# The second GEMM of the four mlps in seven half-size block products

## The chip, the cores and the metric

The kernel runs on one core of a Trainium2 chip. The metric is the device time of one execution in microseconds (us), the median of the runs shown; lower is better.

## The reference

The program is two transformer-like blocks, one after the other, over 512 tokens of width 1024 in float32. The first has latent attention, a gated linear attention, a merge and a convolutional FFN. The second has four layers, each with a mixer and then a squared-ReLU mlp, and these four mlps are what the change touches:

```python
def _sqrelu_mlp(h, w1, w2):
    return jnp.square(jax.nn.relu(h @ w1)) @ w2

def second_block(x, ...):
    for i in range(DEPTH_2):
        ...
        x = x + mix
        x = x + _sqrelu_mlp(_rmsnorm(x, norm_mlp_g[i]), mlp_w1[i], mlp_w2[i])
    return _rmsnorm(x, final_norm_g)
```

DEPTH_2 is 4, h is 512 x 1024, w1 is 1024 x 4096 and w2 is 4096 x 1024.

## The kernel before

Everything is held with features on the 128 partitions and tokens along the free axis. The residual x stays in SBUF as eight tiles of 128 features x 512 tokens.

Every float32 matmul is made as three matmuls on rounded parts. An operand v is split in a high part hi, rounded by a cast on ScalarE (ACT), and a low part lo = v - hi, made by VectorE (DVE); mm3 (L97 to L101) then adds hi*hi, hi*lo and lo*hi into one PSUM bank. One such matmul has a 128 x 128 stationary operand (a tile of weights) and 512 tokens as the moving one. Weights arrive as raw panels of 128 x 1024 float32 (512 KB) by a DMA of the SP queue into wraw (three buffers), and are split in whi (L83, ACT) and wlo (L85, DVE), three buffers each. `split` (L173 to L182) does the same for activations.

The mlp (L994 to L1026) of one layer goes in four quarters (q), each of 1024 of the 4096 hidden columns. A quarter has a first GEMM of eight column tiles (m), each with one w1 panel and 8 x 3 matmuls; a tile is taken out of PSUM by `evict`: DVE multiplies max(ps, 0) by the norm's factor rb (L1006, tile h), ACT squares it (L1007) and `split` makes its parts hh and hl. Then comes the second GEMM of the quarter, eight column tiles of the output, each with one w2 panel (8 k tiles x 128 columns) and 8 x 3 matmuls with the quarter's eight hh, hl; DVE adds the bank to the tile of x (L1022). In the last quarter of a layer `residual` (L956 to L963) makes that addition (L960) and, for the tile, the operand xh, xl of the next mixer (ACT L948, DVE L949), the square (ACT L191) and its addition to acc_x, on GpSimd (POOL, L194) for all tiles but the last. The last layer makes no operand. GpSimd has no other work in the mlps.

The order of the instructions in each engine's queue is fixed when the program is built, by a framework that sees the dependencies and the buffers; it may put an instruction ahead of one that the code writes before it. There are no due times or costs in the code.

## Time and profile before

| | us |
|---|---|
| median of 3 runs | 3118.34 |
| lowest and highest run | 3111.39, 3121.61 |
| span of the profiled execution, first to last instruction | 3113.3 |
| TensorE (PE) busy in that span | 3029.7 (97%) |
| VectorE (DVE) busy | 1784.0 (57%) |
| ScalarE (ACT) busy | 1222.5 (39%) |
| GpSimd (POOL) busy | 292.5 (9%) |

The profiled execution's own time is its span and what lies around it, which the profile does not show; the median of the runs is 5.0 us above the span. A matmul's record is longer than the distance to the next one, since matmuls are pipelined: where the pace matters, starts are compared. The granted clock is given in shares of TensorE's full speed.

### The profile page before, as it was taken

The numbers are of one execution on the slowest core, as the hardware profiler recorded it, in microseconds if no ns is written. First come the engines' busy times: TensorE is split into PE (matmuls) and PEld (weight loads), VectorE is DVE, ScalarE is ACT, GpSimd is POOL, SyncE is SP. The second block draws the span as 40 slices with busy tenths as digits, with TensorE's granted clock in tenths as the row PEclk, the third lists the DMA queues.
The fourth block names the chain that finished last, engine by engine and source line by source line (L and its number), as shares of the span: only waits on it lengthen the run. The fifth ranks groups of instructions, "written<-read, shape, count | busy, mean of one in ns | idle before, by whom it ended". The sixth has DMA issues, their size and how long they took to land.

```text
span 3113.3 us, 34927 instructions
## 1 busy us (share of the span) xinstructions
PE 3029.7 (97%) x13740; PEld 2493.1 (80%) x13740; DVE 1784.0 (57%) x2444; ACT 1222.5 (39%) x1725; POOL 292.5 (9%) x197
## 2 busy tenths in 40 slices
PE   7999999899999999999999999999999999999998
PEld 4878778678888778888888888888888887788886
DVE  7758795598944974443445344455543459744443
ACT  5336653433333654322344222322322246642222
POOL 3212310100001210000101000100100012100001
PEclk8999999999999999999999999999999999999999
DMA  5571234433332523233322323332233224333322
GB/s 200 190 239 55 80 110 137 168 100 97 95 98 85 137 87 110 95 96 101 109 88 91 99 95 96 101 95 95 95 96 101 95 95 129 91 107 100 96 95 75
DMA packets 108932, 336.67 MB, mean 108 GB/s; under 512 B 12096, under 2 KB 18624, under 8 KB 107744
## 3 DMA queue, kind: packets, MB, share of 16 engines
q1 hardware_dynamic: 99568, 318.13, 32.2%
q10 hardware_dynamic: 9200, 16.32, 1.6%
q8 instruction: 107, 1.75, 0.2%
q14 instruction: 57, 0.47, 0.0%
HBM read 314.22 MB, written 13.63 MB: 105 GB/s over the span
## 4 chain that ended last, share of the span: by engine, by line
PE 79%; DVE 7%; ACT 2%; issue 1%; POOL 1%; DMA 0%; SPq 0%; ACTq 0%; DVEq 0%; POOLq 0%
PE ps L101 25%; PE ps L99 25%; PE ps L100 25%; DVE xc L1094 1%; DVE wlo L85 1%; PE po L120 1%; DVE xc L1168 0%; ACT whi L83 0%; PE pu L766 0%; PE pt L649 0%; DVE tg L1166 0%; PE ps L120 0%; POOL sg L854 0%; POOL yl L182 0%; DVE xc L1167 0%
## 5 line engine op out<-in xcount | busy, mean ns | idle before, releaser
L83 ACT CAST whi<-wraw 128x1024 fp32r<-128x1024 f32 (+3 forms) x523 | 535.4, 1025 | 1492.6 <-PE ps L100 1319.7
L99 PE MATMUL ps<-xh,whi 128*128 128x512 f32 x2224 | 874.6, 395 | 10.1 <-ACT xh L346 6.6
L101 PE MATMUL ps<-xh,wlo 128*128 128x512 f32 x2224 | 875.0, 394 | 5.8 <-DVE wlo L85 5.0
L100 PE MATMUL ps<-xl,whi 128*128 128x512 f32 x2224 | 873.2, 393 | 2.8 <-DVE xl L351 2.8
L85 DVE TENSOR_TENSOR wlo<-wraw,whi 128x1024 fp32r<-128x1024 f32 (+3 forms) x513 | 613.6, 1196 | 244.1 <-ACT whi L83 238.4
L99 PEld LDWEIGHTS ps<-xh,whi 128*128 128x128 f32 x2224 | 421.6, 190 | 97.9 <-ACT xh L346 6.8
L101 PEld LDWEIGHTS ps<-xh,wlo 128*128 128x128 f32 x2224 | 421.1, 189 | 97.5 <-DVE wlo L85 8.5
L100 PEld LDWEIGHTS ps<-xl,whi 128*128 128x128 f32 x2224 | 421.6, 190 | 89.8 <-DVE xl L351 3.5
L101 PE MATMUL ps<-hh,wlo 128*128 128x512 f32 x1200 | 467.2, 389 | 0.0
L100 PE MATMUL ps<-hl,whi 128*128 128x512 f32 x1200 | 467.2, 389 | 0.0
L99 PE MATMUL ps<-hh,whi 128*128 128x512 f32 x1200 | 467.2, 389 | 0.0
L1006 DVE SCALAR_TENSOR_TENSOR h<-ps,rb 128x512 f32<-128x512 f32 x128 | 88.1, 691 | 321.4 <-PE ps L101 321.4
L194 POOL TENSOR_TENSOR acc_x<-acc_x,sq 128x512 f32<-128x512 f32 x54 | 87.5, 1620 | 1959.6 <-ACT sq L191 1959.6
L99 PEld LDWEIGHTS ps<-hh,whi 128*128 128x128 f32 x1200 | 225.3, 188 | 46.8
L100 PEld LDWEIGHTS ps<-hl,whi 128*128 128x128 f32 x1200 | 225.3, 188 | 46.6
L101 PEld LDWEIGHTS ps<-hh,wlo 128*128 128x128 f32 x1200 | 225.3, 188 | 46.5
L1022 DVE TENSOR_TENSOR x<-ps,x 128x512 f32<-128x512 f32 x96 | 66.4, 692 | 314.2 <-PE ps L101 314.2
L101 PE MATMUL ps<-yh,wlo 128*128 128x512 f32 x360 | 140.9, 392 | 3.9 <-DVE wlo L85 3.9
L99 PE MATMUL ps<-yh,whi 128*128 128x512 f32 x360 | 140.9, 391 | 0.8 <-DVE sg L853 0.5
L100 PE MATMUL ps<-yl,whi 128*128 128x512 f32 x360 | 140.8, 391 | 0.4 <-DVE yl L182 0.4
L960 DVE TENSOR_TENSOR x<-ps,x 128x512 f32<-128x512 f32 x64 | 44.2, 691 | 163.0 <-PE ps L101 162.8
L907 DVE SCALAR_TENSOR_TENSOR cacc<-pad,vecs,cacc 128x512 f32<-128x512 f32 x176 | 131.5, 750 | 4.3
(401 smaller groups left out, 3140.9 us busy)
## 6 DMA issues: line engine op xcount, KB each, us to landing
wraw<-in_w SPq DMA_DIRECT2D x256, 512.0 KB, 3.5
wraw<-in_w_up SPq DMA_DIRECT2D x44, 512.0 KB, 3.4
wraw<-in_a_w_in SPq DMA_DIRECT2D x40, 512.0 KB, 3.5
wraw<-in_w_ada SPq DMA_DIRECT2D x32, 512.0 KB, 3.9
wraw<-in_w_in SPq DMA_DIRECT2D x29, 512.0 KB, 3.5
wraw<-in_c_w_in SPq DMA_DIRECT2D x24, 512.0 KB, 3.4
wraw<-in_a_w_out SPq DMA_DIRECT2D x32, 320.0 KB, 2.8
adaw<-in_w_ada SPq DMA_DIRECT2D x8, 1024.0 KB, 9.4
```

Source lines behind the costliest of these rows:

```text
L83: nc.scalar.copy(hi[:, :n], raw[:, :n])
L85: e.tensor_tensor(lo[:, :n], raw[:, :n], hi[:, :n].bitcast(F32), ALU.subtract)
L99: mm(out, wh, xh, start=start, stop=False)
L100: mm(out, wh, xl, start=False, stop=False)
L101: mm(out, wl, xh, start=False, stop=stop)
L120: ops = [self.nc.tensor.matmul(*o, start=i == 0, stop=i == last) for i, o in enumerate(ops)]
L194: (nc.vector if k == last else eng or nc.gpsimd).tensor_tensor(acc, acc, s, ALU.add)
L907: nc.vector.scalar_tensor_tensor(av, src, w, av, ALU.mult, ALU.add)
L960: nc.vector.tensor_tensor(xm, ps, xm, ALU.add)
L1006: nc.vector.scalar_tensor_tensor(h, ps, 0.0, self.rb, ALU.max, ALU.mult)
L1022: nc.vector.tensor_tensor(self.x[:, m, :], ps, self.x[:, m, :], ALU.add)
L1094: nc.vector.scalar_tensor_tensor(xm, t[:, k:k + T], w(k), xm, ALU.mult, ALU.add)
```

## The change

The second GEMM of a quarter is made in pairs of output column tiles (m, m + 1). For such a pair the output is a 2 x 2 block matrix: two column tiles by two halves of 256 tokens. The quarter's eight k tiles make four k-pairs, an even and an odd tile, and so w2 is a 2 x 2 block of two k halves by two column tiles. Strassen's scheme in Winograd's form makes the four output blocks of seven block products in place of eight. A block product (`product`) is four k-pairs x 3 matmuls of 256 tokens.

- Operands of the activations (`quad`): from the two tiles of a k-pair, cut into four halves H, four differences t are made on GpSimd (one behind the even tile, three behind the odd one); seven blocks (B11, T1, B21, B22, T3, T2, T4) are split into hh and hl by ACT and DVE.
- Operands of the weights (`Feed`): from the two raw panels a and b of a pair GpSimd makes four sums of 512 columns (`sum`, tile ssum, one buffer). Split are panel a (chunk 0), ssum's first half (chunk 1), its second half (chunk 2), and the second half of panel b (the tail, tiles thi and tlo). w2 is laid out on the host with the even k tiles ahead of the odd ones.
- Evictions (`pair`): three PSUM banks A, E and D. Three partial results are copied to SBUF (u) by ACT; GpSimd adds u to x in two steps ("u", 512 columns, and "d", 256), and DVE adds four banks of 256 columns to x.
- `Feed.pump` writes the loads and splits of coming panels behind each tile or product; the first pair of a quarter goes through its products in the order 1526374, the others in 1265734.
- In a layer's last quarter `residual` is called for both tiles behind each pair, without an addition of its own.

```diff
+TH = T // 2
+EVEN_ODD = [0, 2, 4, 6, 1, 3, 5, 7]
+B11, T1, B21, B22, T3, T2, T4 = range(7)
...
+class Feed:
+    USES = {"1": (0, 0), "2": (0, 1), "6": (1, 0), "5": (1, 1), "7": (2, 0), "3": (2, 1), "4": (3, 0)}
+    LEFT = {0: "12", 1: "65", 2: "73"}
...
+    def pump(self):
+        k, nc = self.k, self.k.nc
+        moved = True
+        while moved:
+            moved = False
+            if self.loaded < len(self.order) and self.loaded - self.read < k.raw_bufs:
+                n, src = self.order[self.loaded]
+                t = k.wp.tile([P, PANEL], F32, tag="wraw", name=k.nm("wraw"), bufs=k.raw_bufs)
+                nc.sync.dma_start(t, src)
+                self.raw.setdefault(n, []).append(t)
+                self.loaded += 1
+                moved = True
+                continue
+            if self.made < len(self.chunks):
+                n, c = self.chunks[self.made]
+                pair = self.items[n][0] == "pair"
+                if len(self.raw.get(n, ())) == (2 if pair else 1) and (
+                        self.made < k.hl_bufs or self.made - k.hl_bufs in self.freed):
+                    if pair and c == 0:
+                        self.sum(n)
+                    src = self.raw[n][0] if c == 0 else self.sums[n][:, 2 * c - 2:2 * c, :].rearrange("p s c -> p (s c)")
+                    hi = k.wp.tile([P, PANEL], F32R, tag="whi", name=k.nm("whi"), bufs=k.hl_bufs)
+                    lo = k.wp.tile([P, PANEL], F32R, tag="wlo", name=k.nm("wlo"), bufs=k.hl_bufs)
+                    k.split(hi, lo, src)
+                    self.got[n, c] = (self.made, hi, lo)
+                    self.made += 1
+                    if not pair:
+                        self.read += 1
+                    moved = True
+                    continue
+            if self.tails and self.tail_free and self.got.get((self.tails[0], 2)):
+                n = self.tails.pop(0)
+                hi, lo = [self.pool.tile([P, 512], F32R, tag=t, name=k.nm(t), bufs=1) for t in ("thi", "tlo")]
+                k.split(hi, lo, self.raw[n][1][:, 512:])
+                self.got[n, 3] = (None, hi, lo)
+                self.tail_free = False
+                self.read += 2
+                moved = True
+    def sum(self, n):
+        k = self.k
+        t = self.sums[n] = self.pool.tile([P, 4, 512], F32, tag="ssum", name=k.nm("ssum"), bufs=1)
+        a, b = self.raw[n]
+        tt = lambda o, x, y, op: k.nc.gpsimd.tensor_tensor(t[:, o, :], x, y, op)
+        tt(1, b[:, :512], b[:, 512:], ALU.add)
+        tt(0, t[:, 1, :], a[:, :512], ALU.subtract)
+        tt(2, a[:, :512], b[:, :512], ALU.subtract)
+        tt(3, a[:, 512:], t[:, 0, :], ALU.subtract)
...
+    def done(self, p):
+        self.used.add(p)
+        for c, ps in self.LEFT.items():
+            if p in ps and self.used.issuperset(ps):
+                self.freed.add(self.got[self.at, c][0])
+        if p == "4":
+            self.tail_free = True
+        if len(self.used) == 7:
+            self.used = set()
+            self.at += 1
...
+    def quad(self, hi, lo, H, pool, part):
+        nc = self.nc
+        t = self.quad_t = pool.tile([P, 4, TH], F32, tag="qt", name=self.nm("qt"), bufs=1) if part == 0 else self.quad_t
+        sub = lambda i, a, b: nc.gpsimd.tensor_tensor(t[:, i, :], a, b, ALU.subtract)
+        if part == 0:
+            sub(0, H[:, 1, :], H[:, 0, :])
+            self.split(hi[:, B11, :], lo[:, B11, :], H[:, 0, :])
+            self.split(hi[:, T1, :], lo[:, T1, :], t[:, 0, :])
+        else:
+            sub(2, H[:, 3, :], t[:, 0, :])
+            sub(1, H[:, 3, :], H[:, 1, :])
+            sub(3, H[:, 2, :], t[:, 2, :])
+            self.split(hi[:, B21:B22 + 1, :], lo[:, B21:B22 + 1, :], H[:, 2:4, :])
+            self.split(hi[:, T3:T4 + 1, :], lo[:, T3:T4 + 1, :], t[:, 1:4, :])
+    def product(self, ps, w, ops, i, start):
+        wh, wl = w
+        mm, last = self.nc.tensor.matmul, len(ops) - 1
+        for j, (xh, xl) in enumerate(ops):
+            c = slice(j * P, (j + 1) * P)
+            mm(ps, wh[:, c], xh[:, i, :], start=start and j == 0, stop=False, skip_group_check=not start)
+            mm(ps, wh[:, c], xl[:, i, :], start=False, stop=False, skip_group_check=not start)
+            mm(ps, wl[:, c], xh[:, i, :], start=False, stop=j == last, skip_group_check=not start)
+    def pair(self, feed, ops, psp, pool, put, first=False):
+        nc = self.nc
+        A, E, D = [self.bank(psp)[:, :TH] for _ in range(3)]
+        u = pool.tile([P, 3, TH], F32, tag="u", name=self.nm("u"), bufs=2)
+        plan = {"1": (A, B11, True), "2": (E, B21, True), "6": (A, T2, False), "5": (D, T1, True),
+                "7": (A, T3, False), "3": (D, B22, False), "4": (A, T4, False)}
+        for p in "1526374" if first else "1265734":
+            ps, i, start = plan[p]
+            self.product(ps, feed.weights(p), ops, i, start)
+            feed.pump()
+            if p == "1":
+                nc.scalar.copy(u[:, 0, :], A)
+            elif p == "6":
+                nc.scalar.copy(u[:, 1, :], A)
+                put("u", None, u[:, 0:2, :])
+            elif p == "5":
+                nc.scalar.copy(u[:, 2, :], D)
+                put("d", None, u[:, 2, :])
+            elif p == "2":
+                put("11", E, u[:, 0, :])
+            elif p == "7":
+                put("22", A, u[:, 2, :])
+            elif p == "3":
+                put("12", D, u[:, 1, :])
+            else:
+                put("21", A, None)
+            feed.done(p)
...
     def residual(self, m, ps, g, pool, last=False):
         nc = self.nc
         xm = self.x[:, m, :]
-        nc.vector.tensor_tensor(xm, ps, xm, ALU.add)
+        if ps is not None:
+            nc.vector.tensor_tensor(xm, ps, xm, ALU.add)
         if not last:
             self.operand(m, g)
         self.sq_last = self.sq_add(self.acc, m, KD - 1, xm, pool, T, apart=last)
...
     def mlp(self, i, psp, sp, g_next):
-        nc, A, tc = self.nc, self.A, self.tc
+        nc, A = self.nc, self.A
         with self.pool(name="ml", bufs=1) as mp:
+            w2 = lambda m, q: A["w2"][i, m, :, q * PANEL:(q + 1) * PANEL]
+            feed = Feed(self, mp, [it for q in range(4) for it in
+                                   [("panel", A["w1"][i, 8 * q + m]) for m in range(8)]
+                                   + [("pair", w2(m, q), w2(m + 1, q)) for m in range(0, 8, 2)]])
+            feed.pump()
             for q in range(4):
-                hs = []
+                ops = []
                 for m in range(8):
-                    pan = self.panel_k(A["w1"][i, 8 * q + m], KD)
-                    ps = psp.tile([P, 512], F32, tag="mm", name=self.nm("ps"))
-                    self.gemm(ps, pan, self.xh, self.xl, KD)
-
-                    def evict(ps=ps, hs=hs):
-                        h = mp.tile([P, T], F32, tag="h32", name=self.nm("h32"), bufs=3)
+                    hi, lo = feed.panel()
+                    ps = self.bank(psp)
+                    self.gemm(ps, [(hi, lo, k * P) for k in range(KD)], self.xh, self.xl, KD)
+                    feed.pump()
+                    def evict(ps=ps, m=m, ops=ops):
+                        if m % 2 == 0:
+                            self.H = mp.tile([P, 4, TH], F32, tag="H", name=self.nm("H"), bufs=2)
+                            ops.append([mp.tile([P, 7, TH], F32R, tag=t, name=self.nm(t), bufs=4) for t in ("hh", "hl")])
+                        h = self.H[:, 2 * (m % 2):2 * (m % 2) + 2, :].rearrange("p a t -> p (a t)")
                         nc.vector.scalar_tensor_tensor(h, ps, 0.0, self.rb, ALU.max, ALU.mult)
                         nc.scalar.activation(h, h, AF.Square)
-                        hh = mp.tile([P, T], F32R, tag="hh", name=self.nm("hh"), bufs=16)
-                        hl = mp.tile([P, T], F32R, tag="hl", name=self.nm("hl"), bufs=16)
-                        self.split(hh, hl, h)
-                        hs.append((hh, hl))
+                        self.quad(*ops[-1], self.H, mp, m % 2)
                     self.when(evict)
                     self.step()
-                for m in range(8):
-                    hi, lo = self.panel(A["w2"][i, m, :, q * PANEL:(q + 1) * PANEL], PANEL)
-                    ps = psp.tile([P, 512], F32, tag="mm", name=self.nm("ps"))
-                    for k in range(8):
-                        ks = slice(k * P, (k + 1) * P)
-                        self.mm3(ps, hi[:, ks], lo[:, ks], hs[k][0], hs[k][1], k == 0, k == 7)
-                    if q < 3:
-                        nc.vector.tensor_tensor(self.x[:, m, :], ps, self.x[:, m, :], ALU.add)
-                    else:
-                        self.residual(m, ps, g_next(m) if g_next else None, sp, last=g_next is None)
+                    feed.panel_done()
+                for m in range(0, 8, 2):
+                    x = self.x[:, m:m + 2, :].rearrange("p m (h t) -> p (m h) t", h=2)
+                    def put(what, ps, u, x=x):
+                        if what == "u":
+                            nc.gpsimd.tensor_tensor(x[:, 0:2, :], x[:, 0:2, :], u, ALU.add)
+                        elif what == "d":
+                            nc.gpsimd.tensor_tensor(x[:, 3, :], x[:, 3, :], u, ALU.add)
+                        else:
+                            n = ("11", "12", "21", "22").index(what)
+                            nc.vector.tensor_tensor(x[:, n, :], ps, x[:, n, :], ALU.add)
+                    self.pair(feed, ops, psp, mp, put, first=m == 0)
+                    if q == 3:
+                        for mm in (m, m + 1):
+                            self.residual(mm, None, g_next(mm) if g_next else None, sp, last=g_next is None)
...
-    A["w2"] = np.stack([_tiles(a["mlp_w2_2"][j]) for j in range(4)])
+    w2 = np.stack([_tiles(a["mlp_w2_2"][j]) for j in range(4)])
+    A["w2"] = w2.reshape(4, 8, P, 4, 8, P)[:, :, :, :, EVEN_ODD].reshape(w2.shape)
```

The first GEMM, the mixers and the first block are as before.

## Rows read from the trace of the kernel before

**Rows 1.** The page's busy times: us, share of the span, instructions.

```profile
PE 3029.7 (97%) x13740; PEld 2493.1 (80%) x13740; DVE 1784.0 (57%) x2444; ACT 1222.5 (39%) x1725; POOL 292.5 (9%) x197
```

**Rows 2.** Stretches of layer 0's mlp: second GEMM, first GEMM, the layer's last second GEMM.

```profile
core 0: us, PE busy (x) PEld busy (x) DVE busy (x) ACT busy (x) POOL busy (x), PEclk, DMA share, GB/s
...
1239.60:1283.10 43.50, 43.50 (x193) 36.06 (x192) 15.33 (x16) 8.44 (x8) 0.00 (x0) 1.00 0.31 97
1283.10:1326.60 43.50, 43.50 (x193) 36.05 (x193) 20.55 (x24) 17.66 (x24) 0.00 (x0) 1.00 0.30 97
...
1500.70:1544.20 43.50, 43.50 (x193) 36.05 (x193) 22.46 (x26) 17.60 (x24) 10.75 (x6) 1.00 0.37 122
```

**Rows 3.** Instruction groups by shape, the weight load: count, busy us, mean ns.

```profile
L99 PEld LDWEIGHTS ps<-hh,whi 128*128 128x128 f32 x1200 | 225.3, 188 | 46.8
```

**Rows 4.** Timeline of PE, one second-GEMM tile's first matmul and the next's.

```profile
1239.62 0.39 PE L99 MATMUL ps<-hh,whi 128*128 128x512 f32 x1
...
1245.07 0.39 PE L99 MATMUL ps<-hh,whi 128*128 128x512 f32 x1
```

**Rows 5.** Timeline of PE, first and last of 24 matmuls of 256 columns.

```profile
170.53 0.28 PE L99 MATMUL ps<-ch,whi 128*128 128x256 f32 x1
...
173.29 0.28 PE L101 MATMUL ps<-ch,wlo 128*128 128x256 f32 x1
```

**Rows 6.** Timeline of all engines around the end of a first-GEMM tile.

```profile
1212.40 1.06 ACT L83 CAST whi<-wraw 128x1024 fp32r<-128x1024 f32 x1 [3.20 <-PE ps L100]
1212.42 0.39 PE L99 MATMUL ps<-xh,whi 128*128 128x512 f32 x1
...
1212.62 0.69 DVE L1006 SCALAR_TENSOR_TENSOR h<-ps,rb 128x512 f32<-128x512 f32 x1 [2.70 <-PE ps L101]
...
1213.35 0.63 ACT L1007 ACTIVATE h<-h 128x512 f32<-128x512 f32 x1
1213.49 1.23 DVE L85 TENSOR_TENSOR wlo<-wraw,whi 128x1024 fp32r<-128x1024 f32 x1 [0.17 <-ACT whi L83]
...
1214.01 0.62 ACT L176 CAST hh<-h 128x512 fp32r<-128x512 f32 x1
```

**Rows 7.** Instruction groups by shape, ACT.

```profile
L83 ACT CAST whi<-wraw 128x768 fp32r<-128x768 f32 x12 | 10.1, 838 | 26.2 <-PE ps L100 24.4 <-issue 0.9 <-ACT stage L426 0.5
...
L652 ACT CAST Th<-pt 128x256 fp32r<-128x256 f32 x32 | 12.0, 377 | 0.0
```

**Rows 8.** Instruction groups by shape, DVE.

```profile
L1022 DVE TENSOR_TENSOR x<-ps,x 128x512 f32<-128x512 f32 x96 | 66.4, 692 | 314.2 <-PE ps L101 314.2
...
L653 DVE TENSOR_TENSOR Tl<-pt,Th 128x256 fp32r<-128x256 f32 x32 | 13.2, 413 | 0.2
```

**Rows 9.** Timeline of POOL: an addition of 512 columns, eight of 256.

```profile
1157.55 1.28 POOL L194 TENSOR_TENSOR acc_x<-acc_x,sq 128x512 f32<-128x512 f32 x1 [5.54 <-ACT sq L191]
...
78.62 6.16 POOL L340 TENSOR_TENSOR xa<-xa,acc 128x256 f32<-128x256 f32 x8 [14.86 <-ACT acc L163]
```

**Rows 10.** Timeline of all engines in layer 3's mixer, DVE and POOL.

```profile
2620.20 1.56 POOL L182 TENSOR_TENSOR yl<-xc,yh 128x512 fp32r<-128x512 f32 x1 [15.90 <-ACT yh L176]
...
2620.52 0.68 DVE L1089 TENSOR_TENSOR xpad<-ps,rb 128x512 f32<-128x512 f32 x1
...
2621.12 1.72 DVE L85 TENSOR_TENSOR wlo<-wraw,whi 128x1024 fp32r<-128x1024 f32 x1
```

**Rows 11.** Timeline of all engines in layer 0's last second GEMM.

```profile
1513.83 0.75 DVE L949 SCALAR_TENSOR_TENSOR xl<-x,vecs,xh 128x512 fp32r<-128x512 f32 x1
...
1513.94 1.78 POOL L194 TENSOR_TENSOR acc_x<-acc_x,sq 128x512 f32<-128x512 f32 x1 [3.66 <-ACT sq L191]
```

**Rows 12.** Timelines of POOL and of DVE in one stretch of the first block.

```profile
52.13 11.63 POOL L317 TENSOR_TENSOR adas<-adas,adaw 128x512 f32<-128x512 f32 x7 [1.30 <-ACT adaw L316]
...
54.40 6.89 DVE L314 SCALAR_TENSOR_TENSOR adas<-adaw,s,adas 128x512 f32<-128x512 f32 x4
```

**Rows 13.** DMA issues: count, KB each, median us to landing.

```profile
wraw<-in_w SPq DMA_DIRECT2D x256, 512.0 KB, 3.5
```

More of the change, by code (lines that the diff above doesn't have):

```diff
@@ L50, with __init__, panel, panel_done @@
 NV = _n
+class Feed:
+    USES = {"1": (0, 0), "2": (0, 1), "6": (1, 0), "5": (1, 1), "7": (2, 0), "3": (2, 1), "4": (3, 0)}
+    LEFT = {0: "12", 1: "65", 2: "73"}
+    def __init__(self, k, pool, items):
+        self.k, self.pool, self.items = k, pool, items
+        self.loaded, self.read = 0, 0
+        self.chunks = []
+        for n, it in enumerate(items):
+            self.chunks += [(n, c) for c in ((0, 1, 2) if it[0] == "pair" else (0,))]
+        self.made, self.freed = 0, set()
+        self.order = [(n, s) for n, it in enumerate(items) for s in it[1:]]
+        self.raw, self.sums, self.got = {}, {}, {}
+        self.lastsum = -1
+        self.tails = [n for n, it in enumerate(items) if it[0] == "pair"]
+        self.tail_free = True
+        self.at, self.used = 0, set()
+    def pump(self):
[45 more added lines that the diff above has]
+        tt(3, a[:, 512:], t[:, 0, :], ALU.subtract)
+    def panel(self):
+        i, hi, lo = self.got[self.at, 0]
+        return hi, lo
+    def panel_done(self):
+        self.freed.add(self.got[self.at, 0][0])
+        self.at += 1
+    def weights(self, p):
+        c, h = self.USES[p]
+        _, hi, lo = self.got[self.at, c]
+        s = slice(512 * h, 512 * h + 512)
+        return hi[:, s], lo[:, s]
+    def done(self, p):
[4 more added lines that the diff above has]
+        if p == "4":
+            self.tail_free = True
+        if len(self.used) == 7:
+            self.used = set()
+            self.at += 1
```

## The prediction

> **What bounds the kernel now.** I read the page's busy table first, then the stretches of one mlp layer, then the instructions around one tile's end. TensorE has work for 97% of the span [rows 1]. The four mlps are where the change lies. In layer 0 one quarter's second GEMM takes 43.50 us, the next first GEMM 43.50 us; layer 0's last second GEMM, with the residual work added, is 43.50 us too [rows 2]. In all three TensorE is busy throughout at a granted clock of 1.00, the upper level of 2.4 GHz; VectorE (DVE) has 15 to 22 us of work there, ScalarE (ACT) 8 to 18, GpSimd (POOL) none or 10.75. So in the mlps the matmul stream is the bound, with no gap. What counts is the time from start to start, not the length of a record: 24 matmuls of 512 columns take 5.45 us, 0.2267 us each [rows 4], while a record lasts 0.39; a weight load of 188 ns [rows 3] fits below it.
>
> **What falls away.** Per quarter (one of 16: four layers of four) the second GEMM has 8 x 8 x 3 = 192 matmuls of 512 columns: 192 x 0.2267 = 43.5 us, as [rows 2] shows. Afterwards it is 4 pairs x 7 products x 4 k-pairs x 3 = 336 matmuls of 256 columns. The trace has such a stream: 23 steps of 256 columns, each with a weight load of its own, take 173.29 - 170.53 = 2.76 us, 0.120 us each [rows 5]. So the load, longer than a step, still doesn't set the pace. 336 x 0.120 = 40.3 us: 3.2 us less per quarter, **-51 us** in all. A product is 1.44 us, a pair 10.08.
>
> The Trainium skill ("TensorE: Matmul & The Clock Gate", Back-to-back issue gap) puts the gap at the columns over 2.4 GHz plus some 2.5 ns. By it the steps would be 216 and 109 ns (estimates from that page) and the gain 663 - 587 = 76 us; both rows lie above it, by 11 ns each, and since matmuls of half the width are twice as many, the row takes 25 us off the gain. The rows decide.
>
> **What is added, and where it can hide.** ACT has 8.44 + 17.66 = 26 us per quarter now [rows 2]; 12 copies u out of PSUM (0.38, as the 128x256 copy in [rows 7]) add 4.6, casts of 3.5 panels per pair in place of 2 (1.05) 6.3, operands of 7 x 256 columns for 4 x 256 some 4: 41 of 84 us. DVE has 36 [rows 2]; six more lo of a panel (1.23, [rows 6]) 7.4, operands some 5, sixteen additions of half a tile (0.41, as the 128x256 row of [rows 8]) for eight of 0.69 another 1: 49. Both stay below TensorE, so by busy share alone they are hidden. POOL goes from next to nothing to 16 subtractions of 256 columns (0.77 each), 16 sums of 512 (1.28), 4 x (u 1.28, d 0.77): 41 us [rows 9]. The w2 layout is made on the host; DMAs stay 512 KB and land in 3.5 us [rows 13]; of eight PSUM banks a pair holds three. These cost nothing as long as that slack stands.
>
> What is not free is DVE and POOL side by side. In [rows 10] POOL's subtraction starts at 2620.20 and ends at 2621.76; DVE's xpad (one operand in PSUM) runs beside it in its usual 0.68; the wlo that follows (both operands in SBUF) is issued at 2621.12 and ends at 2622.84, 1.08 us after POOL's end. The reverse is in [rows 11]: POOL, issued 0.11 us behind an SBUF-SBUF operation of DVE, takes 1.78 in place of 1.28. In [rows 12] seven POOL additions need 11.63 us, and four DVE operations among them 6.89: 1.72 us for one of each. They take turns. The Trainium skill ("SBUF — State Buffer", Who interferes with whom) says so: GpSimd's SBUF reads and VectorE's second SBUF operand share one port, and the second to issue is held until the first ends. The trace agrees, and this is the rule that speaks against the change.
>
> So I count turns. A pair needs of POOL 4 x 1.28 (sums) + 1.28 + 0.77 = 7.2 us, of DVE three lo of 1024 (1.08) and one of 512 (0.44, the 1.72 less 1.28) = 3.7. In sum 10.9, some 0.3 less with handovers overlapped as in [rows 12]: I take 10.6, against 10.08 of TensorE. The additions out of PSUM don't count. The first GEMM has room (per two tiles 3.1 of POOL and some 4 of DVE in 10.9 us), and there the first pair is made in advance.
>
> *Start of a second GEMM.* Let 0 be the start of its first matmul; [rows 6] has the same moment at 1212.42. ACT casts the panel whose buffer comes free (there at 1212.40), DVE's h comes, ACT's square ends at 1.56, the cast's lo on DVE runs from 1.07 to 2.2. POOL's three subtractions for the last operands need H complete: 1.6, held to 2.2 by that lo; ended at 3.0; held by the lo of B21 and B22 to 3.5; ended at 5.0. Then ACT's cast of three parts (0.84, [rows 7]) to 5.9, and its lo on DVE, 0.86 (three quarters of 1.14, as 1024 columns start to start), behind a POOL operation that has begun meanwhile: 7.6. The fourth product (T2) wants the last k-pair's lo at 3 x 1.44 + 9 x 0.12 + 0.12 = 5.5. Stall 2.1 us, x 16 = **+34**. Bounds: 0.3 with no turns (1.6 + 2.3 + 0.84 + 0.86 + gaps), 3.4 if a coming panel's cast and lo are put ahead: +5 to +54. B21's lo, ready at 3.5, is wanted at 4.0: hidden.
>
> *The pairs.* The sum buffer is single, so sum n+1 starts when chunk 2 of n is split. Chunk 2 of pair 1 is ready at about 15.8; then one pair per 10.6: pair 3's at 37.0. Its fifth product wants it at 3 x 10.08 + 4 x 1.44 + 2.1 = 38.1. It holds, with 1.1 us to spare: **0**. Bounds 0 to +2 per quarter (12 quarters, +24).
>
> *The last quarter of a layer.* Here come per pair two POOL additions of squares (1.28) and two DVE xl (0.44 to 0.6): 3.5 us of turns; before the change they had POOL idle around them [rows 2, 11]. The residuals of pairs 0 and 1 fall before pair 3's chunk 2: 7.0 - 1.1 = 5.9 us of stall; in the last layer, which makes no operand, 5.1 - 1.1 = 4.0. 3 x 5.9 + 4.0 = **+22**; bounds 0 (they run after the last sum) to twice that, +43.
>
> **Sum.** -51 + 34 + 0 + 22 = +5 on the profiled span of 3113.3: 3118. The median of the runs, 3118.34, lies 5.0 above that span; I add it: **3122 us**. A change of 0.3%, 9 us, is about what a measurement of this kernel can tell from none.
>
> **Rivals.**
> *The turns fall into gaps* (faster). If POOL's work finds DVE idle (DVE is needed 49 of 84 us) and the additions of squares wait behind the last sum, the stall at the start shrinks to some 0.8 and the last quarter costs nothing: -51 + 13 = -38, 3080 to 3090. For it: the budget is over by only 5%, and [rows 12] is the densest place of the trace. Against: both directions of [rows 10, 11]. It decides where a pair's turns come below 10.08.
> *The single sum buffer* (slower). Nothing uses the port while ACT casts chunk 2 (1.06 and a hand-over), and the next sum waits: 11.9 per pair, chunk 2 of pair 3 at 39.6, 1.5 us of stall in 12 quarters and 2.5 more in 4: +28, 3150. It decides above 11.2 per pair.
> *The queues as written* (much slower). If the second raw panel of pair n+1 is fetched only after the tail of n is split, the chain is 3.5 (DMA) + 5.1 (sums) + 2.1 (u, d) + additions and two lo, near 15: 8 us a quarter, +126, 3245. Against: in [rows 6] a coming panel's cast stands ahead of the eviction, so queues are ordered by what is ready.
> *A narrow step at half the wide one* (faster), 0.2267 / 2 = 0.113 in place of 0.120: 5376 x 0.0066 = 36 us more gain on TensorE, but turns bound the pairs, so that about 20 of it would be seen: 3100. Against: [rows 5]. The page's gap, 109 ns, goes the same way.
>
> **Chances.** The sum as it stands (3105 to 3140) 0.35; gaps 0.30; sum buffer 0.24; queues as written 0.08; half step 0.03. Faster: 0.30 + 0.03 + 0.02 of the first; same: 0.21 of it; slower: 0.24 + 0.08 + 0.12 of it. The bounds give -51 + 5 = -46 (3072) to -51 + 54 + 24 + 43 = +70 (3188); the range is 3075 to 3190, the likeliest case's own 3105 to 3140.
>
> **What would show it.** Right: steps of 0.120 in the products; a gap of about 2 us before the fourth product of each quarter, ended by DVE's lo; POOL's busy time up from 292 [rows 1] by 650 us or more, 512-column sums well above 1.28 on the mean, DVE's lo of 1024 above 1.23; last quarters some 5 us longer than the others. Wrong: no gaps, sums at 1.3; or TensorE waiting in every pair for a lo made from ssum; or a step of 256 columns away from 0.120, which would move the whole sum by 5.4 us per ns.

## The result and the profile after

The changed kernel takes 3283.0 us (median of 4 runs, 3280.9 to 3285.5) against 3117.6 for the kernel before: a ratio of 1.0531, 95% interval 1.0516 to 1.0546. The forecast was 3122 us, its range ended at 3190: the size was off by 161 us. Of the three signs, slower had been given the largest chance, 0.44.

The page's busy times of the kernel after answer to [rows 1]; line numbers are now those of the changed kernel:

```profile
PE 3049.4 (93%) x16044; PEld 2597.7 (79%) x16044; DVE 2140.6 (65%) x2828; ACT 1452.8 (44%) x2173; POOL 1142.1 (35%) x837
```

TensorE's share fell from 97% to 93%: a gap has opened, while VectorE and GpSimd are far from full on the mean. The stretches, as in [rows 2], are the four second GEMMs of layer 0 and the last one of layer 3, each from its first product to the next block's first matmul:

```profile
core 0: us, PE busy (x) PEld busy (x) DVE busy (x) ACT busy (x) POOL busy (x), PEclk, DMA share, GB/s
1236.83:1289.31 52.48, 43.27 (x337) 40.98 (x336) 32.82 (x38) 22.67 (x34) 34.92 (x24) 1.00 0.25 79
1332.86:1384.44 51.58, 43.00 (x338) 40.92 (x336) 31.44 (x37) 22.30 (x34) 34.90 (x24) 1.00 0.26 81
1427.99:1479.55 51.56, 43.03 (x338) 40.95 (x337) 31.37 (x37) 22.30 (x34) 34.88 (x24) 1.00 0.27 81
1523.09:1582.96 59.87, 48.32 (x338) 46.06 (x336) 40.76 (x43) 30.30 (x48) 43.05 (x29) 0.89 0.23 69
3207.45:3264.55 57.10, 47.07 (x337) 44.88 (x335) 29.98 (x35) 24.04 (x39) 42.05 (x30) 0.91 0.10 28
```

Each was 43.5 before. The other layers repeat this: the twelve quarters that are not a layer's last sum to 623.0 us, 100.8 more than 12 x 43.52; the four last ones to 236.8, 62.7 more. That is 163.4 of the 165.7 us by which the profiled spans differ (3279.0 - 3113.3); the first GEMMs are as long as before.

The list of waits, with TensorE's product lines (engine, line, what it waited for: us, times, longest) and the links behind them:

```profile
PE ps L223 <- DVE x L1194: 63.5, 57, 3.7
PE ps L223 <- ACT u L242: 44.2, 16, 2.8
PE ps L224 <- DVE hl L342: 24.7, 48, 0.8
...
DVE x L1194 <- POOL x L1191: 43.9, 47, 3.1
POOL ssum L123 <- DVE wlo L342: 61.1, 27, 3.5
ACT whi L336 <- POOL ssum L123: 61.6, 20, 3.4
```

L1194 is a block's addition out of PSUM, L242 the copy u1, L1191 the addition "d", L1189 "u", L123 the sums, L336 and L342 the casts and the lo parts. The wait that the forecast put first, on hl at the start, is the smallest of these three. TensorE's list has no wait for a lo part made from ssum, the one for which the forecast had looked in the pairs.

**One quarter from the inside**, the second of layer 0. TensorE's matmuls that waited:

```profile
1334.52 0.39 PE L224 MATMUL ps<-hl,whi 128*128 128x256 f32 x1 [0.30 <-DVE hl L342]
1338.03 0.39 PE L224 MATMUL ps<-hl,whi 128*128 128x256 f32 x1 [0.39 <-DVE hl L342]
1340.18 0.38 PE L223 MATMUL ps<-hh,whi 128*128 128x256 f32 x1 [0.57 <-ACT hh L336]
1341.37 0.39 PE L224 MATMUL ps<-hl,whi 128*128 128x256 f32 x1 [0.80 <-DVE hl L342]
1346.06 0.39 PE L223 MATMUL ps<-hh,whi 128*128 128x256 f32 x1 [2.76 <-ACT u L242]
1349.65 0.39 PE L223 MATMUL ps<-hh,thi 128*128 128x256 f32 x1 [1.30 <-DVE x L1194]
1360.71 0.38 PE L223 MATMUL ps<-hh,thi 128*128 128x256 f32 x1 [1.19 <-DVE x L1194]
```

Counted from start to start less the step of 0.12, the first four are 0.46 + 0.55 + 0.73 + 1.06 = 2.8 us: the start that was forecast at 2.1. The fifth, 2.92, is product 7, which adds into bank A and must wait until the copy u1 has read it. The others are product 4 of each pair (its weights are thi), which adds into A after "22" has read it: 1.46, 1.35, 1.08, 0.51, 4.4 in sum. With 40.3 of steps this makes 50.4 of 51.58; the rest is in gaps under 0.25.

Why is A read so late? ScalarE, GpSimd and VectorE in the same quarter:

```profile
1344.69 1.04 ACT L336 CAST whi<-ssum 128x1024 fp32r<-128x1024 f32 x1 [3.35 <-POOL ssum L123]
1345.64 0.36 ACT L242 COPY u<-ps 128x256 f32<-128x256 f32 x1
```

```profile
1350.80 1.30 POOL L123 TENSOR_TENSOR ssum<-wraw 128x512 f32<-128x512 f32 x1 [2.00 <-DVE wlo L342]
1352.06 1.75 POOL L123 TENSOR_TENSOR ssum<-wraw,wraw 128x512 f32<-128x512 f32 x1
1353.77 1.29 POOL L123 TENSOR_TENSOR ssum<-ssum,wraw 128x512 f32<-128x512 f32 x1
1355.14 2.16 POOL L123 TENSOR_TENSOR ssum<-wraw,ssum 128x512 f32<-128x512 f32 x1
1357.26 1.27 POOL L1189 TENSOR_TENSOR x<-x,u 128x512 f32<-128x512 f32 x1
1358.49 1.71 POOL L1191 TENSOR_TENSOR x<-x,u 128x256 f32<-128x256 f32 x1
1362.20 1.29 POOL L123 TENSOR_TENSOR ssum<-wraw 128x512 f32<-128x512 f32 x1 [2.00 <-DVE wlo L342]
```

```profile
1360.23 0.76 DVE L1194 TENSOR_TENSOR x<-ps,x 128x256 f32<-128x256 f32 x2 [0.62 <-POOL x L1191]
1360.90 1.21 DVE L342 TENSOR_TENSOR wlo<-ssum,whi 128x1024 fp32r<-128x1024 f32 x1
```

The copy u1 stands on ScalarE behind a cast that waits 3.35 us for a sum. On GpSimd the next pair's four sums stand ahead of this pair's u and d. "22" adds to the same quarter of x as d and waits for it; behind "22" and "12" stands chunk 2's lo part, and that frees the one sum buffer, for which the next sums wait. It is a ring: 11.40 us from one pair's first sum to the next's, 1350.80 to 1362.20, where the products need 10.08.

### The profile page after: what moved, and what is told of

Its sections match the earlier page's. It is cut to its first block, busy times and chain, and to the rows that moved or that the text cites. A ratio compares the mean times of both kernels' runs of the same rounds, so it can differ in the third digit from the quotient of the medians.

```text
span 3279.0 us, 41343 instructions
## 1 busy us (share of the span) xinstructions
PE 3049.4 (93%) x16044; PEld 2597.7 (79%) x16044; DVE 2140.6 (65%) x2828; ACT 1452.8 (44%) x2173; POOL 1142.1 (35%) x837
## 4 chain that ended last, share of the span: by engine, by line
PE 48%; POOL 22%; DVE 10%; ACT 5%; issue 5%; DMA 2%; POOLq 0%; DVEq 0%; SPq 0%; ACTq 0%
PE ps L259 13%; PE ps L260 13%; PE ps L261 13%; POOL ssum L123 13%; POOL qt L204 3%; POOL x L1189 2%; POOL x L1191 2%; PE ps L223 2%; DMA wraw<-in_w 2%; DVE wlo L342 2%; PE ps L224 2%; PE ps L225 1%; DVE H L1176 1%; ACT H L1177 1%; DVE x L1194 1%
## 5 line engine op out<-in xcount | busy, mean ns | idle before, releaser
L259 PE MATMUL ps<-xh,whi 128*128 128x512 f32 x2224 | 872.7, 394 | 10.6 <-ACT xh L506 5.8
L185 ACT CAST whi<-wraw 128x1024 fp32r<-128x1024 f32 (+2 forms) x267 | 265.1, 995 | 563.9 <-PE ps L260 404.7
L223 PE MATMUL ps<-hh,whi 128*128 128x256 f32 x1536 | 451.5, 294 | 55.8 <-ACT u L242 44.2
L224 PE MATMUL ps<-hl,whi 128*128 128x256 f32 x1536 | 447.2, 291 | 24.7 <-DVE hl L342 24.7
L225 PE MATMUL ps<-hh,wlo 128*128 128x256 f32 x1536 | 441.0, 287 | 0.0
L187 DVE TENSOR_TENSOR wlo<-wraw,whi 128x1024 fp32r<-128x1024 f32 (+2 forms) x257 | 299.8, 1166 | 194.8 <-ACT whi L185 193.3
L336 ACT CAST whi<-wraw 128x1024 fp32r<-128x1024 f32 (+1 forms) x208 | 208.1, 1004 | 251.3 <-PE ps L260 160.9
L342 DVE TENSOR_TENSOR wlo<-wraw,whi 128x1024 fp32r<-128x1024 f32 (+1 forms) x208 | 275.3, 1325 | 66.3 <-ACT whi L336 66.3
L342 DVE TENSOR_TENSOR wlo<-ssum,whi 128x1024 fp32r<-128x1024 f32 x128 | 188.2, 1470 | 77.8 <-ACT whi L336 77.6
L204 POOL TENSOR_TENSOR qt<-H 128x256 f32<-128x256 f32 x128 | 135.8, 1061 | 282.6 <-ACT H L1177 282.6
L342 DVE TENSOR_TENSOR hl<-qt,hh 128x256 fp32r<-128x256 f32 (+1 forms) x128 | 93.2, 728 | 183.5 <-ACT hh L336 183.5
L336 ACT CAST whi<-ssum 128x1024 fp32r<-128x1024 f32 x128 | 133.9, 1046 | 167.6 <-POOL ssum L123 61.6
L336 ACT CAST hh<-qt 128x256 fp32r<-128x256 f32 (+1 forms) x128 | 79.3, 620 | 268.9 <-POOL qt L204 268.9
```

Of the source, the lines that this page charges most:

```text
L185: nc.scalar.copy(hi[:, :n], raw[:, :n])
L187: e.tensor_tensor(lo[:, :n], raw[:, :n], hi[:, :n].bitcast(F32), ALU.subtract)
L204: sub = lambda i, a, b: nc.gpsimd.tensor_tensor(t[:, i, :], a, b, ALU.subtract)
L223: mm(ps, wh[:, c], xh[:, i, :], start=start and j == 0, stop=False, skip_group_check=not start)
L224: mm(ps, wh[:, c], xl[:, i, :], start=False, stop=False, skip_group_check=not start)
L225: mm(ps, wl[:, c], xh[:, i, :], start=False, stop=j == last, skip_group_check=not start)
```

## The experiments

Kernels e1 to e17 are the changed kernel with edits; "before" was timed beside each on the same chip. Two columns give the length of a quarter in us, read from TensorE's timeline as above: the third and the last of layer 1 (layers are counted from 0). Where the next tile's matmuls are mixed into the last quarter, it can't be read so (-).

```
                            us      ratio [95%]                third  last
before                    3117.6                               43.5   43.5
changed                   3283.0  1.0531 [1.0516, 1.0546]      51.57  59.89
e1_puts_dve               3228.1  1.0356 [1.0341, 1.0372]      46.84  53.65
e2_copies_first           3279.8  1.0522 [1.0504, 1.0539]      52.34  59.87
e3_no_sums                3137.1  1.0063 [1.0048, 1.0078]      44.72  45.00
e4_ssum2                  3259.4  1.0455 [1.0437, 1.0472]      50.62  56.48
e5_puts_copies            3261.1  1.0463 [1.0445, 1.0480]      49.59  55.55
e6_sums_dve               3184.6  1.0219 [1.0202, 1.0236]      46.85  50.81
e7_sums_copies_quad       3162.3  1.0147 [1.0125, 1.0170]      45.32  48.66
e8_bank4                  3104.9  0.9970 [0.9954, 0.9987]      41.05  46.97
e9_order_pool_sums        3172.8  1.0181 [1.0168, 1.0195]      44.55  54.01
e10_acc_dve               3091.3  0.9924 [0.9910, 0.9938]      41.05  -
e11_first_order           3098.4  0.9944 [0.9931, 0.9956]      40.71  46.45
e12_classic_last          3091.8  0.9925 [0.9912, 0.9937]      41.06  43.52
e13_shadow_sums           3282.3  1.0535 [1.0518, 1.0553]      52.69  58.22
e14_best_strassen         3083.4  0.9899 [0.9884, 0.9913]      40.72  -
e15_best_mixed            3086.8  0.9908 [0.9893, 0.9922]      40.72  43.52
e16_shadow_clean          3230.6  1.0358 [1.0342, 1.0373]      48.30  55.26
e17_all_quads             3086.6  0.9900 [0.9884, 0.9917]      40.72  -
```

**e1, u and d off GpSimd's queue.**

```diff
 if what == "u":
-    nc.gpsimd.tensor_tensor(x[:, 0:2, :], x[:, 0:2, :], u, ALU.add)
+    nc.vector.tensor_tensor(x[:, 0:2, :], x[:, 0:2, :], u, ALU.add)
 elif what == "d":
-    nc.gpsimd.tensor_tensor(x[:, 3, :], x[:, 3, :], u, ALU.add)
+    nc.vector.tensor_tensor(x[:, 3, :], x[:, 3, :], u, ALU.add)
```

> The two additions of copied products to x ("u", "d") go from GpSimd to VectorE; nothing else changes. Theory A (order in the queues): block "22" reads bank A only after "d", and "d" stands on GpSimd behind the four sums of the next pair; with it gone from that queue, TensorE's waits on VectorE's L1194 before product 4 (64 us of PE's, 1.0 to 1.5 us in each pair after the first) nearly vanish: 3215 to 3240 us. Theory B (the two engines only take turns at SBUF, their work adds up): the sum of the work is the same, so 3270 to 3300 us, and the waits only change their names.

3228.1 us, 55 us less: in theory A's range. But the run does not part order from length, as theory B's "the sum of the work is the same" did not hold. On the mean u and d took 1.65 and 1.28 us on GpSimd and take 1.23 and 0.70 on VectorE: 1.0 us a pair less, some 63 us in 64 pairs. A kernel with u and d ahead of the next sums on GpSimd, order alone, was not run. The waits on L1194 fell from 63.5 to 34.9 us rather than to nothing: d now stands on VectorE, behind lo parts.

**e2 and e5, the copy u1 ahead of the cast.** e2 moves the copies in the code; e5 is e1 with the order stated as well:

```diff
+    if p in "165":
+        self.ucopy = nc.scalar.copy(u[:, "165".index(p), :], D if p == "5" else A)
     feed.pump()
-    if p == "1":
-        nc.scalar.copy(u[:, 0, :], A)
...
-    k.split(hi, lo, src)
+    cast = k.split(hi, lo, src)
+    if k.ucopy is not None:
+        k.after(k.ucopy, cast)
```

> ScalarE's copies of banks A and D (u0, u1, u2) are issued before the casts of the weight chunks that the same product frees, instead of behind them. Theory A: the wait of 2.8 us before product 7 of every quarter's first pair (44 us in 16 quarters) is a copy of 0.38 us that stands behind a cast which waits for a sum; it goes, and 25 to 45 us come back: 3238 to 3258 us. Theory B (the sums themselves are late, whoever waits for them): the next product waits for the same chunk instead, under 12 us come back.

> As e1_puts_dve, and with the copies of banks held ahead of the casts by a stated order on ScalarE (e2 changed only where the code writes them, and the order that was built kept u1 behind the cast). Theory A: with u1 out from behind the cast that waits for a sum, the 2.0 to 2.15 us before product 7 of a quarter's first pair go, 32 us in 16 quarters: 3195 to 3205 us, if nothing else is late there. Rival (chunk 1 of the next pair is late by as much): 3218 to 3230 us.

e2 changed nothing, because ScalarE's order did not change: its timeline (the copies are now L240) still has the cast that waits ahead of u1:

```profile
1338.10 1.04 ACT L337 CAST whi<-ssum 128x1024 fp32r<-128x1024 f32 x1 [3.34 <-POOL ssum L123]
1339.05 0.36 ACT L240 COPY u<-ps 128x256 f32<-128x256 f32 x1
```

e5 missed: 33 us slower than e1. The wait on u1 is gone, but the cast of the first pair's chunk 2 now stands behind copies too. Its lo part frees the sum buffer later, and the next sum starts 9.4 us into the second quarter (1344.60 - 1335.24), 6.4 in e1. Chunk 1's lo part waits for that sum, and "22" stands behind it on VectorE:

```profile
1351.04 1.33 DVE L347 TENSOR_TENSOR wlo<-ssum,whi 128x1024 fp32r<-128x1024 f32 x1 [2.27 <-ACT whi L341]
1352.29 0.74 DVE L1200 TENSOR_TENSOR x<-ps,x 128x256 f32<-128x256 f32 x2
```

From the next pair on the sums wait for transfers: 125 of the 181 us that they wait in e5, against 20 in the changed kernel. So with sums on GpSimd one late place passes its lateness to the next; removing the wait on u1 did not bring what it showed.

**e3, no sums; e4, two sum buffers.**

```diff
# e3
-    if pair and c == 0:
-        self.sum(n)
-    src = self.raw[n][0] if c == 0 else self.sums[n][:, 2 * c - 2:2 * c, :].rearrange("p s c -> p (s c)")
+    src = self.raw[n][0] if c == 0 else self.raw[n][c - 1]
# e4
-    t = self.sums[n] = self.pool.tile([P, 4, 512], F32, tag="ssum", name=k.nm("ssum"), bufs=1)
+    t = self.sums[n] = self.pool.tile([P, 4, 512], F32, tag="ssum", name=k.nm("ssum"), bufs=2)
```

> Leaves out GpSimd's four sums of weight blocks per pair; chunks 1 and 2 are split from the raw panels instead, so the casts, the lo parts, the transfers and all matmuls stay (the output is not the reference's). Theory A and B alike: what is left is the start of each quarter (2.1 to 2.8 us, 16 of them), and the last quarters' residual work: 3150 to 3185 us. Theory C (most of the excess is the start stall, the quads and the clock): 3230 us or more, as the sums are not what product 4 and 7 wait for.

> The sums get two buffers. The ring as read from the trace (sums, u, d, the block puts, chunk 2's lo part, which frees the buffer: 11.4 us for a pair of 10.1) is opened at its last link; the order in GpSimd's queue stays. Theory A, ring by way of the buffer: a pair falls to 10.1 to 10.5 us in the first three quarters: 3220 to 3250 us. Rival (GpSimd's own queue is the ring: sums 6.4, u 1.3, d 1.7, with turns at the port): a pair stays over 11 us, 3265 to 3285 us.

e3, which leaves the sums out, fell below the expected range: 146 of the 166 us go. The start of a quarter shrinks from 2.8 to 1.1 us, and the last quarters, whose residual work is all still there, cost 0.3 us more than the others in place of 8.3. Yet e3 is still slower than the kernel before, at 44.7 us a quarter: "22" out of A costs 0.5 us a pair even so.

e4 brought 23.6 us, between its two expectations: the buffer is one link of the ring, and opening it leaves u and d behind the sums. In its second quarter the wait before product 7 is gone and those before product 4 fell from 4.4 to 3.2 us, but the start grew from 2.8 to 4.7: the second pair's sums now stand on GpSimd ahead of the last k-pair's differences.

**e6 to e9, where the sums are made, and the order around them.** Each adds to the one before; e9 is e8 with the sums back on GpSimd and u and d on VectorE.

```diff
# e6
-    tt = lambda o, x, y, op: k.nc.gpsimd.tensor_tensor(t[:, o, :], x, y, op)
+    tt = lambda o, x, y, op: k.nc.vector.tensor_tensor(t[:, o, :], x, y, op)
# e7: the copies' order as in e5, and the differences of a quarter's last tile
-    sub = lambda i, a, b: nc.gpsimd.tensor_tensor(t[:, i, :], a, b, ALU.subtract)
+    sub = lambda i, a, b: (nc.vector if last else nc.gpsimd).tensor_tensor(t[:, i, :], a, b, ALU.subtract)
# e8: product 4 in a bank F
-    A, E, D = [self.bank(psp)[:, :TH] for _ in range(3)]
+    A, E, D, F = [self.bank(psp)[:, :TH] for _ in range(4)]
...
     put("22", A, u[:, 2, :])
+    put("21", A, None)
...
-    put("21", A, None)
+    put("21", F, None)
```

> The four sums of a pair on VectorE in place of GpSimd; u and d stay on GpSimd, everything else as in the changed kernel. GpSimd keeps 2 us of work per pair, so d is no longer behind sums. VectorE has 6.0 us of lo parts and block additions per pair by the durations without turns, and gets four additions of 0.7: 8.8 of 10.1. Theory A, with turns at the port as what lengthens the queue: 3160 to 3200 us. Rival (VectorE's single queue becomes the bound, since lo parts now stand behind sums that wait for transfers): 3230 to 3300 us.

> As e6, with the copies held ahead of the casts, and the three differences of a quarter's last tile on VectorE (three at 0.4 us in place of 2.85 us in series on GpSimd). Theory A: the start of a quarter loses 1.6 us of its 2.8 and the copy's wait: 30 to 60 us under e6, 3120 to 3150 us. Rival: the start is bound by the casts and lo parts, under 10 us from e6.

> As e7, with product 4 in a fourth PSUM bank of its own, so that it waits for no block addition; block 21 is then added in two steps (one more VectorE addition of 0.41 us per pair). Theory A: the wait before product 4, some 0.5 us a pair even with no sums, goes: 25 to 40 us under e7. Rival (VectorE is full; the next pair's chunk is late instead): within 10 us of e7, or above it.

> All the ordering mends of e8 (copies ahead of casts, the last tile's differences on VectorE, product 4 in its own bank) but the sums back on GpSimd, with u and d on VectorE. It parts the two things that e6 moved at once. Order alone (theory A): a sum is ready in time wherever it is made, so near e8: 3105 to 3135 us. Length and turns (an addition of 512 columns takes 1.3 us on GpSimd and up to 2.2 in turns, and stretches a lo part from 1.2 to 2.0): the pair stays over 10.8 us: 3150 to 3210 us.

e6 hit: 98 us less than the changed kernel. e7 missed its range by 12 us but had the sign. In e8 the wait before product 4 is gone and a quarter runs at 41.05 us: 40.3 of steps, and one wait of 0.65 on hl at the start. The gain over e7, 57 us, is more than the 25 to 40 expected: e7's quarters, at 42.9 to 45.3 us, fell to 41.05 to 41.47, and the last ones by 1.7 to 4.2. e8 is the first version below the kernel before, by 0.3%.

e9 says that the mends of e8 are not all: with them, and u and d in the sums' place on VectorE, e9 still takes 68 us more than e8. The sums still end waits there (ScalarE's casts of chunks waited 175 us for them), so e9 does not show turns alone.

**e13 and e16, turns alone.** e8's sums stay on VectorE and are made a second time on GpSimd; nothing reads the second set.

```diff
     tt(3, a[:, 512:], t[:, 0, :], ALU.subtract)
+    t2 = self.pool.tile([P, 4, 512], F32, tag="shadow", name=k.nm("shadow"), bufs=1)
+    gg = lambda o, x, y, op: k.nc.gpsimd.tensor_tensor(t2[:, o, :], x, y, op)
+    gg(1, b[:, :512], b[:, 512:], ALU.add)
+    gg(0, t2[:, 1, :], a[:, :512], ALU.subtract)
+    gg(2, a[:, :512], b[:, :512], ALU.subtract)
+    gg(3, a[:, 512:], t2[:, 0, :], ALU.subtract)
...
-    nc.gpsimd.tensor_tensor(x[:, 0:2, :], x[:, 0:2, :], u, ALU.add)
+    pass
...
-    nc.gpsimd.tensor_tensor(x[:, 3, :], x[:, 3, :], u, ALU.add)
+    pass
```

> As e8 (sums on VectorE), with the four sums of each pair made a second time on GpSimd, into a tile that nothing reads; u and d, GpSimd's other work in these quarters, are left out (the output is not the reference's). Nothing waits for GpSimd's results, so in quarters 0 to 2 only its turns at SBUF, and its hold on the raw panels, can cost. Read by quarters 0 to 2, 41.05 us each in e8 and 44.55 in e9. Turns alone explain e9: 43.5 us or more. The sums' lateness explains it: 41.0 to 41.8 us.

> As e13, with all differences of the operands on VectorE. In e13 a difference that the quarter's start needs stood on GpSimd behind the second set of sums, so something did wait for GpSimd: 3.9 us of the start. Now GpSimd's queue holds nothing in quarters 0 to 2 that anyone waits for (u and d are left out, as in e13, so that the output is not the reference's). Read by quarters 0 to 2 (e8: 41.05 us). Turns alone: 43.5 to 47 us, VectorE's additions at 1.4 to 1.8 us in place of 0.68. If e13's loss was the queue: 41 to 42 us.

e13 was not a clean test: a difference of the operands stood on GpSimd behind the second sums, and TensorE waited for it. In e16 no engine in quarters 0 to 2 waits for a result of GpSimd, and they take 48.1 to 50.1 us in place of 41.05 to 41.47. First e8, then e16, a third quarter each:

```profile
1399.21:1440.26 41.05, 40.56 (x337) 40.35 (x336) 36.63 (x54) 20.96 (x31) 14.39 (x8) 1.00 0.28 89
```

```profile
1426.08:1474.37 48.29, 42.85 (x338) 41.96 (x337) 45.65 (x57) 21.28 (x33) 17.61 (x11) 0.96 0.26 77
```

VectorE's busy time grew by 9 us for nearly the same instructions; a small part of the longer quarter is the clock (0.96), lower after the waits; three of e16's twelve such quarters have no step at the lower clock and still take 48.2 to 48.3. Its timeline and GpSimd's, same stretch of e16:

```profile
1445.90 1.78 DVE L125 TENSOR_TENSOR ssum<-wraw,wraw 128x512 f32<-128x512 f32 x1
1447.61 1.78 DVE L125 TENSOR_TENSOR ssum<-ssum,wraw 128x512 f32<-128x512 f32 x1
1449.31 2.32 DVE L354 TENSOR_TENSOR wlo<-wraw,whi 128x1024 fp32r<-128x1024 f32 x1
1451.56 0.68 DVE L125 TENSOR_TENSOR ssum<-wraw,ssum 128x512 f32<-128x512 f32 x1
```

```profile
1445.39 1.75 POOL L131 TENSOR_TENSOR shadow<-wraw,wraw 128x512 f32<-128x512 f32 x1
1447.10 1.74 POOL L131 TENSOR_TENSOR shadow<-shadow,wraw 128x512 f32<-128x512 f32 x1
1448.92 1.63 POOL L131 TENSOR_TENSOR shadow<-wraw,shadow 128x512 f32<-128x512 f32 x1
```

An addition that VectorE makes in 0.68 us alone (the fourth) takes 1.78 beside GpSimd, a lo part 2.32 in place of 1.21, and both engines step at one pace. The raw panels, which GpSimd holds longer here, show little: VectorE's sums waited 12.6 us for transfers in the whole of e16. Both sets of sums take turns here, more than in the changed kernel: e16 shows that turns alone can cost this much, not what they cost there.

**e10 to e12, the last quarter and the start; e14, e15, e17, put together.**

```diff
# e10: additions of squares in residual, after the products
-    self.sq_add(self.acc, m, KD - 1, xm, pool, T, apart=last)
+    self.sq_add(self.acc, m, KD - 1, xm, pool, T, eng=nc.vector if ps is None else None, apart=last)
# e11
-    for p in "1526374" if first else "1265734":
+    for p in "1523674" if first else "1265734":
# e12: the items of the last quarter; its loop is that of the kernel before
-    + [("pair", w2(m, q), w2(m + 1, q)) for m in range(0, 8, 2)]])
+    + ([("pair", w2(m, q), w2(m + 1, q)) for m in range(0, 8, 2)] if q < 3 else
+       [("panel", w2(m, q)) for m in range(8)])])
```

e14 is e8 with e10 and e11, e15 is e12 with e11, e17 is e14 with all differences of the operands on VectorE.

> As e8, with the additions of squares in the last quarters on VectorE (two of 0.7 us per pair) in place of GpSimd (2.6 us alone, 4.1 in turns). If turns are what makes e8's last quarters 46.97 us: 45 us or less, 3090 to 3099 us in all. If VectorE's work is (11.8 us a pair then): 47 to 49 us, 3105 to 3115 us.

> As e8, with the first pair of a quarter in the order 1523674, so that the product that needs the last difference (T2) comes one later. Theory: the wait of 0.65 us on hl in e8's product 6 goes, 16 times: 3092 to 3099 us. Rival: product 3 then waits for the lo part of chunk 2 by as much: 3102 to 3112 us.

> As e8 in three quarters of a layer, with the last quarter's second GEMM as in the kernel before (eight products of 512 columns, no sums), where the residual's work meets the sums. By e8's rows a last quarter of 46.97 becomes 43.5, 13.5 us in all: 3086 to 3095 us. If the operands' new layout or the changeover costs a wait, 3098 or more.

> As e8, with e10's squares on VectorE and e11's order of the first pair. If both gains stand beside each other: 3091 - 6.5 = 3084 us, within 4. If they meet in the last quarter's VectorE queue: 3089 to 3093 us.

> As e12 (last quarter of each layer as before the change), with e11's order of the first pair in the other three. By rows 0.33 us in each of 12 quarters: 3086 to 3090 us; if nothing adds up, 3092.

> As e14, with all differences of the operands on VectorE in place of GpSimd, not only those of a quarter's last tile. In the first GEMM GpSimd is hidden either way: 3080 to 3086 us, no change from e14 (3083). If tile 6's difference was late at a quarter's start or stretched VectorE's lo parts there: 3076 to 3080.

e10 and e11 hit in total (13.6 and 6.5 us under e8), e12 too; the one last quarter of e10 that can be read as above, layer 3's, fell from 46.6 to 43.8 us. The two ways to mend a last quarter, squares on VectorE or no Strassen there, are worth the same. e14 adds both gains: 3083.4 us, 1.0% faster than the kernel before (0.9884 to 0.9913). Its third quarter, 40.72, is little more than the steps. e15 and e17, some 3 us above it, are no different within the spread of the runs: in the first GEMMs GpSimd is hidden.

## Why the prediction was wrong

**The steps, -51: right.** 0.120 us per matmul of 256 columns held; e14's quarters of 40.71 are 336 of them and 0.4 us.

**The start, +34: right in kind, 45 in size.** Four waits, 2.8 us in place of one of 2.1, ended by hh and hl, within the bounds (+5 to +54). Much of it is the sums': in e3 1.1 us is left.

**The pairs, "It holds ... 0": this step failed.** It measured (2.92 + 4.40 + 1.16) x 16 = 136 us, by the quarter read above, where the bounds ended at +24. The price of turns in it was nearly right: I had 10.6 us per pair, and the ring takes 11.4. GpSimd's six instructions of a pair run from 1350.80 to 1360.20, 9.4, in place of the 7.2 they would take alone; "22" and "12" (0.76), which I had not counted, follow, and then the lo part. Two things were missing.

First, I asked only when chunk 2 would be ready, for which TensorE's list of waits has no entry, and called PSUM free: "of eight PSUM banks a pair holds three", "the additions out of PSUM don't count". But bank A takes four of the seven products, and three of them must wait until someone else has read it: product 6 for the copy of product 1, product 7 for u1, product 4 for "22". The last two are TensorE's largest waits, and e8, which gives product 4 a bank, takes 57 us off e7.

Second, I laid the queues out by what is ready. The rival "The queues as written" had u, d, the additions and the lo parts in one chain, 8 us a quarter, 3245 us; I gave it 0.08, because in [rows 6] a cast stands ahead of an eviction. Yet each queue's order is fixed, and a later pair's instruction may stand in front: the next sums before d, a cast that waits for a sum before u1. e1, two additions on another queue and engine, gave 55 us back. That rival was nearest, with a wrong head: the ring closes through the sum buffer, and a transfer ended only 20 us of the sums' waits. (Where the ring is opened elsewhere, transfers do come: 47 us in e4, 125 in e5, 76 in e9.)

**The single sum buffer, +28 in its rival:** opening it in e4 brought 23.6 us. The rival had the place. That the price is near is partly luck: it was charged to chunk 2's lo part, for which TensorE does not wait, and e4's gain is what is left after the longer start.

**The last quarter, +22: 30** (8.3 x 3 + 5.5). The size is near, the reason less than half: e3 shows that the residual's work costs 0.3 us a quarter when no sums run beside it, and more than half of the 30 us is no stall by turns but steps at TensorE's lower clock behind longer waits. By the last section's rows such a step takes 0.093 us more; counted on TensorE's timeline, the four last quarters have about 180 more of them than four ordinary ones, some 17 us (an estimate from these numbers).

With these the sum is -51 + 45 + 136 + 30 = +160, of 165.7 measured on the spans.

The signs that I had named for "right" came: a gap at the start, GpSimd's busy time up by 850 us, sums at 1.43 to 1.93 us and lo parts above 1.23 on the mean, longer last quarters. They test steps and turns; none of them looks at who reads a bank between two products.

**What made it dear** is then shown by pairs of runs. The sums: 146 us go without them (e3). Turns: e16 against e8, 7 to 9 us a quarter with no engine waiting for a result of GpSimd. Who waits for whom: the bank, 57 us (e8 against e7); the buffer, 23.6 (e4); ScalarE's order alone, 33 us, in the wrong direction (e5 against e1). e1's 55 us are order and length together. In e16 the block additions, with one operand in PSUM, take 0.41 us on the mean as in e8, one of them (at 1459.77) in the middle of GpSimd's additions, while additions with both operands in SBUF went from 0.68 to 1.78. This bears out the rule cited ahead (the Trainium skill, "SBUF — State Buffer", Who interferes with whom), also in its exception: a VectorE instruction with one operand in PSUM does not take turns.

How the 136 us split into turns and order can't be told to the microsecond, as each lengthens the other: e5 and e7 show that a wait's size is not the gain from removing it.

## What to carry to other kernels

Before costing extra work on idle engines at nothing, write down who reads each PSUM bank between two products that add into it, and what stands ahead of that reader on its queue; a bank more was worth 57 us here (e8 against e7). Work on GpSimd with operands in SBUF is not beside VectorE's work of that kind but in turn with it: additions of 0.68 us on VectorE cost less there than of 1.3 on GpSimd, even with VectorE at 37 of 41 us. Where one buffer and several queues close a ring, compare the ring's period (11.4) with the bound's (10.08), not the queues' busy shares.

## What the runs showed of the hardware that was not expected

After some long waits TensorE ran at its lower clock, which made the last quarters worse than the waits alone. In layer 0's last quarter of the changed kernel (TensorE's timeline, then three stretches: behind the wait of 2.77 us, behind that of 3.74 us, and after it):

```profile
1536.30 0.58 PE L223 MATMUL ps<-hh,whi 128*128 128x256 f32 x1 [2.77 <-ACT u L242]
1536.68 0.41 PE L224 MATMUL ps<-hl,whi 128*128 128x256 f32 x1
...
1554.11 0.58 PE L223 MATMUL ps<-hh,thi 128*128 128x256 f32 x1 [3.74 <-DVE x L1194]
1554.49 0.41 PE L224 MATMUL ps<-hl,thi 128*128 128x256 f32 x1
...
1557.05 0.41 PE L224 MATMUL ps<-hl,whi 128*128 128x256 f32 x1
```

```profile
1535.80:1539.10 3.30, 2.80 (x13) 2.80 (x14) 1.92 (x2) 0.45 (x2) 3.23 (x2) 0.50 0.38 102
1554.20:1559.20 5.00, 5.00 (x24) 5.00 (x25) 3.44 (x5) 3.10 (x5) 3.33 (x3) 0.50 0.00 0
1559.40:1563.80 4.40, 4.40 (x37) 4.40 (x37) 4.40 (x4) 1.80 (x3) 4.40 (x4) 0.97 0.38 119
```

After 3.74 us without work the granted clock is 0.50, the lower level of 1.2 GHz, for 5 us, and a step takes 0.213 us (twelve in 1557.05 - 1554.49) in place of 0.120; then it is back. The length of the wait does not tell it by itself in these rows: in the second quarter, with a wait of 2.76 us, the stretch shows 1.00 throughout, while the wait of 2.77 us before product 7 in this last quarter has 0.50 behind it, and so has that of layer 1's second quarter (1877.20 to 1883.80). A wait can thus cost more than its length: here 5 us of half speed behind 3.74 of waiting, some 2.2 us more (24 matmuls x 0.093).

Second, the turns in e16's rows were strict: while both engines had additions with all operands in SBUF, VectorE's took 1.78 us and GpSimd's 1.74, one for one, so that the engine whose addition takes about half as long alone (0.68 against 1.28) ran at the other's pace.
